# Counting out background matmuls per round: a constant count against an estimate of the round's other matmul work

## The chip, the cores and the metric

The kernel runs on one core of a Trainium2 chip. The metric is the device time of one execution in microseconds (us). Engines: PE is TensorE, which multiplies matrices (its weight loads are listed as PEld), DVE is VectorE, ACT is ScalarE, POOL is GpSimd, SP issues DMAs.

## What is computed

One layer of a hybrid encoder over 1040 tokens (16 meta tokens and 1024 others) of width 1024. A root-mean-square norm is followed by one input projection to 5920 columns, whose columns feed three branches: neighbourhood attention (8 heads), a chunked gated linear attention (GLA, 4 heads, both directions) and RWKV-7 time mixing (8 heads, both directions). The branches are concatenated, go through one output projection and are added to the input; a last norm follows.

```python
hn = rms_norm(h, norm_g[l])
z_na  = hn @ w[:, :NA_COLS]
z_gla = hn @ w[:, NA_COLS:NA_COLS + GLA_COLS]
z_rw  = hn @ w[:, NA_COLS + GLA_COLS:]
...
h = h + jnp.concatenate([o_na, o_gla, o_rw], axis=-1) @ w_out[l]
```

The RWKV-7 recurrence, per head and direction, is `S = S * w + (S a) b + v k` and `y = S r`, over all tokens in order. The kernel computes it in chunks of 64 tokens.

## The kernel before

**Projection.** The input projection is cut into jobs of 128 columns. A job multiplies in three parts (high and low halves of weights and activations), so that a chunk of some 346 tokens takes 24 matmuls of 128x128 by 128x346 into one PSUM tile named `pj`, and a job with three chunks 72 (one narrow job has 48). `proj_steps` (L209) is a generator that yields after each matmul; after a chunk's last one the evacuation (`evac`) is emitted: one ACT step and, for the RWKV columns, two DVE steps into a tile `zt`, which a DMA then writes to memory. There are 34 jobs before the attention's: first the 14 of the RWKV branch with two of its gates among them, then other gates and the GLA columns. `Feed.pull(n)` (L364) advances the current job by n matmuls; when a job starts, the weights of the job after it are loaded (`weights`, L154). Every seventh matmul it also advances a small normalization (`norm`, tiles `rb` and `nps`).

**Recurrent stage.** `run` (L912) holds seven generators: chain (C), late (L), two inversions (I for full units, J for units of one chunk), rest (R), early (E) and drain. They work on 20 units: 4 pairs of heads times one unit of one chunk and four units of four chunks for each direction. Each pass of the `while` loop is called a round here. In a round every generator advances to its next yield, which emits a few matmuls and the DVE, ACT and POOL work that belongs to them; after it, a number of projection matmuls is pulled. A chain step takes three rounds (tile `c`, with `y` beside it), and one step waits for the one before; an inversion takes 13 rounds of 16 to 36 small matmuls in 16-bit (tiles `fps`, `ta`, `tb`, `eps`, `cps`), each followed by a DVE or ACT step; `late` makes, in two rounds of each unit, the products `g`, which DVE masks into `NT`, `XR` and `GR`.

Before, each of the first 12 rounds pulls 16 matmuls, each later one 8 (`QUOTA`). When the last unit is in `rest`, `swap` (L948) pulls all jobs that are left, closes the pools of the early part and replaces the jobs by three of the attention's.

**Order.** The program's scheduler orders each engine's instructions by the order of emission and by readiness. `place` (L84) adds ordering edges: a projection matmul pulled after round r stands behind the main matmuls of round r - 2 (`LA = 2`), so that it can move forward by no more than two rounds.

Of the kernel before, what the change touches and what calls it, by code (L numbers as in the profile page):

```python
# [7 lines left out]
F32 = mybir.dt.float32  # L8
# [5 lines left out]
PM = 1  # L14
YM = 2
LA, LA2, LA3 = 2, 2, 3
QUOTA, NQ, GI, OQ, GP = 8, 5, 0, 6, 1.5
F32R = mybir.dt.float32r
F16 = mybir.dt.float16
BF16 = mybir.dt.bfloat16  # L20
# [10 lines left out]
C = 64  # L31
# [44 lines left out]
def emit(ctx, tc, a, out):  # L76
# [2 lines left out]
    PS = bass.MemoryType.PSUM  # L79
    half = (slice(0, 64), slice(64, 128))  # L80

    lane = {"cur": None, "anchors": (), "seen": None}

    def place(r):  # L84
        if lane["cur"] == "pj":
            for n in lane["anchors"]:
                tc.add_manual_dep(r.ins, n, NOSYNC, reason="issue order")
        lane["seen"] = r.ins.name
        return r

    class Tensor:
        def matmul(self, *args, **kw):
            return place(nc.tensor.matmul(*args, **kw))  # L93

        def transpose(self, *args, **kw):
            return place(nc.tensor.transpose(*args, **kw))  # L96

    def hop(g, name):
        prev, lane["cur"], lane["seen"] = lane["cur"], name, None
        done = next(g, 0) == 0  # L100
        seen, lane["cur"] = lane["seen"], prev
        return done, seen
# [69 lines left out]
    with tc.tile_pool(name="xp", bufs=1) as xp, tc.tile_pool(name="px", bufs=2, space=PS) as px:  # L172
        warm = xp.tile([128, 1], F32, name="warm")
        S.activation(warm, small[:, 0:1], AF.Sqrt)
        rows = [(16, a["meta"])] + [(128, a["x"][t * 128:(t + 1) * 128, :]) for t in range(8)]
# [208 lines left out]
    src = [Feed(jobs)]  # L384
# [17 lines left out]
    nst = {}  # L402
# [337 lines left out]
    seen = {}  # L740
# [168 lines left out]
    past = []  # L909

    HPO = {}
    def run(gens, quota):  # L912
        kinds = {id(g): k for k, g in zip('CLIJRED', gens)}
        while gens:
            alive, marks = [], []
            for g in gens:
                off = HPO.get(kinds[id(g)], 0)
                if off:
                    with tc.high_priority(off):
                        done, seen = hop(g, "main")  # L920
                else:
                    done, seen = hop(g, "main")
                if not done:
                    alive.append(g)
                if seen:
                    marks.append(seen)
            gens = alive
            past.append(marks)
            lane["anchors"] = past[-1 - LA] if len(past) > LA else ()
            if len(past) % PM == 0:  # L930
                src[0].pull(quota * PM if len(past) > 12 else 16, 3 if "pool" in nst else 10 ** 6)

    def seq(*gs):
        for g in gs:
# [27 lines left out]
    ready = {k: -1 for k in "ELRIJC"}  # L962
# [64 lines left out]
    if 1:  # L1027
        lora_weights(0)
    src[0].pull(10 ** 6, FIRST)
    run([stream("C", chains, lambda u: past_("I", u) and past_("R", u)),  # L1030
         stream("L", late, gate_l),
         stream("I", invert, lambda u: past_("L", u)),
# [505 lines left out]
def build(arr):  # L1538
    import concourse.bacc as bacc
    import concourse.tile as tile  # L1540

    nc = bacc.Bacc("TRN2", target_bir_lowering=False, num_devices=1)
    aps = {k: nc.dram_tensor(f"in_{k}_dram", v.shape, mybir.dt.from_np(v.dtype), kind="ExternalInput").ap() for k, v in arr.items()}
    out = nc.dram_tensor("out_0_dram", (T, D), F32, kind="ExternalOutput").ap()
    with tile.TileContext(nc, schedule_with_timeline_sim=True) as tc, ExitStack() as ctx:
        emit(ctx, tc, aps, out)
    return nc
# [9 lines left out]
```

## Time and profile before

| | |
|---|---|
| median of 3 runs | 1490.52 us (1487.98 to 1501.66) |
| the profiled execution's own time | 1485.04 us |
| its span, first to last instruction | 1482.8 us |
| mean granted PE clock | 0.959 of full |
| PE busy | 1375.4 us, 93% of the span |
| DVE, ACT, POOL busy | 886.2, 611.5, 665.7 us |

The recurrent stage begins at about 75 us with its first rounds and its last chain step starts at 974.7 us; attention, GLA and the output projection follow. A busy share is a mean over a stretch. The granted clock is 1.00 where PE ran at full clock all the time and 0.50 where it ran at half.

### The profile page before, as it was taken

What the parts mean: (1) busy time and instruction counts of PE and PEld (TensorE: products, weight loads), DVE (VectorE), ACT (ScalarE), POOL (GpSimd) and SP (SyncE); (2) the same over time, 40 slices, a digit from 0 to 9 for tenths busy, and PEclk for the clock granted to TensorE, in tenths of its full rate; (3) what the DMA queues carried; (4) which work ended last, traced back from release to release, by engine and by line L of the source; (5) the groups of instructions that cost most, each with busy time, mean ns of one, the idle gap of its engine ahead of it and who ended that gap; (6) DMA issues with size and microseconds to landing.
All of it is one profiled execution on the core that took longest, in us unless ns stands there. A gap on an engine that the chain in (4) does not pass through costs nothing. (4 is left out here: it accounts for less than half of the span.)

```text
span 1482.8 us, 36124 instructions
## 1 busy us (share of the span) xinstructions
PE 1375.4 (93%) x14656; PEld 1132.4 (76%) x14656; DVE 886.2 (60%) x1936; ACT 611.5 (41%) x1368; POOL 665.7 (45%) x775
## 2 busy tenths in 40 slices
PE   5888988999899999999999999998999989899997
PEld 4877777877788788788888888776677767667786
DVE  7425465676856565746656564546757577775554
ACT  5324243334443443434334332435465554644333
POOL 6435364464646664657656563223323132321223
PEclk9999898999989999999999999999999999899999
DMA  7655533433433444334333433155353423731432
GB/s 205 162 134 134 133 95 86 123 91 71 117 95 88 113 89 121 86 91 113 87 106 80 100 99 78 44 115 134 84 120 87 112 73 96 240 111 55 132 93 93
DMA packets 184806, 158.88 MB, mean 107 GB/s; under 512 B 19152, under 2 KB 168048, under 8 KB 184640
## 3 DMA queue, kind: packets, MB, share of 16 engines
q1 hardware_dynamic: 119616, 117.12, 26.6%
q0 software_dynamic: 63264, 35.20, 13.2%
q10 hardware_dynamic: 1760, 4.26, 0.8%
q8 instruction: 115, 1.88, 0.5%
q14 instruction: 51, 0.42, 0.1%
HBM read 123.81 MB, written 32.72 MB: 106 GB/s over the span
## 5 line engine op out<-in xcount | busy, mean ns | idle before, releaser
L93 PE MATMUL pj<-hhi,whi 128*128 128x348 f32 (+10 forms) x1088 | 378.9, 349 | 12.4 <-DVE zt L263 8.7
L93 PE MATMUL pj<-hlo,whi 128*128 128x348 f32 (+10 forms) x1088 | 377.0, 347 | 0.0
L93 PE MATMUL pj<-hhi,wlo 128*128 128x348 f32 (+8 forms) x1064 | 368.6, 347 | 1.7 <-POOL wlo L166 1.7
L93 PEld LDWEIGHTS pj<-hhi,whi 128*128 128x128 f32 (+1 forms) x1088 | 212.1, 195 | 28.2 <-issue 11.9
L93 PEld LDWEIGHTS pj<-hlo,whi 128*128 128x128 f32 (+1 forms) x1088 | 212.0, 195 | 12.9 <-issue 2.6
L93 PEld LDWEIGHTS pj<-hhi,wlo 128*128 128x128 f32 x1064 | 208.9, 196 | 14.4 <-issue 2.6
L166 POOL TENSOR_TENSOR wlo<-wraw,whi 128x512 fp32r<-128x512 f32 x94 | 125.6, 1337 | 144.6 <-DMA whi<-in_w_in_dram 53.6
L162 POOL DMA_DIRECT2D whi<-in_w_in_dram x94 | 74.7, 795 | 114.7 <-PE pj L93 101.3
L1219 POOL TENSOR_SCALAR sc<-sc,rc 128x288 f32<-128x288 f32 (+3 forms) x64 | 45.4, 710 | 163.9 <-DVE rc L1218 136.8
L845 POOL TENSOR_TENSOR dS<-SV,dec 64x128 f32<-64x128 f32 x128 | 59.1, 462 | 73.7 <-DVE SV L861 68.3
L699 POOL TENSOR_TENSOR BK<-BK,dec 64x1024 f32<-64x1024 f32 (+1 forms) x40 | 68.4, 1710 | 49.1 <-PE g L93 45.6
L791 ACT CAST XA<-ta 128x512 f16<-128x512 f32 (+1 forms) x92 | 49.9, 542 | 90.5 <-PE ta L93 87.3
L785 DVE TENSOR_TENSOR Fc<-fps,im 128x512 f16<-128x512 f32 (+1 forms) x92 | 58.5, 636 | 47.7 <-PE fps L93 43.6
L93 PE MATMUL ops<-hhi,oh 128*128 128x512 f32 x256 | 86.8, 403 | 0.0
L93 PE MATMUL g<-XR,BK 64*128 64x128 f32 (+1 forms) x544 | 67.6, 296 | 5.5 <-DVE GR L687 5.5
L93 PEld LDWEIGHTS g<-XR,BK 64*128 64x128 f32 x544 | 53.9, 192 | 16.5 <-issue 12.3
L1211 DVE CUSTOM_DVE_ANT_0 sc<-sps,bt 128x288 f32<-128x288 f32 (+3 forms) x64 | 33.3, 520 | 44.8 <-PE sps L93 30.4
L1328 DVE TENSOR_TENSOR yv<-ops,yv 128x512 f32<-128x512 f32 x48 | 33.0, 690 | 41.5 <-PE ops L93 41.3
L93 PEld LDWEIGHTS ops<-hhi,oh 128*128 128x128 f32 x256 | 48.6, 191 | 11.9 <-issue 1.0
L861 DVE TENSOR_TENSOR SV<-c,dS 64x128 f32<-64x128 f32 x128 | 36.7, 286 | 35.0 <-PE c L93 32.6
L257 ACT ACTIVATE zt<-pj,cols 128x347 f32<-128x347 f32 (+1 forms) x42 | 23.0, 549 | 82.5 <-PE pj L93 74.0
L93 PEld LDWEIGHTS <-Nh 64*64 64x64 f16 x1600 | 43.4, 111 | 15.0 <-issue 12.8
(302 smaller groups left out, 3048.7 us busy)
## 6 DMA issues: line engine op xcount, KB each, us to landing
whi<-in_w_in_dram POOLq DMA_DIRECT2D x94, 256.0 KB, 4.0
wraw<-in_w_in_dram SPq DMA_DIRECT2D x94, 256.0 KB
lr<-rwl POOLq DMA_DIRECT2D x32, 256.0 KB, 3.5
rwz<-zt SPq DMA_DIRECT2D x12, 544.0 KB
orr<-oscr SPq DMA_DIRECT2D x96, 64.0 KB
wr<-in_w_out_dram SPq DMA_DIRECT2D x12, 512.0 KB
glz<-zt SPq DMA_DIRECT2D x8, 544.0 KB
k<-rwz SPq DMA_DIRECT2D x32, 128.0 KB
```

What stands on the lines that cost most here:

```text
L93: return place(nc.tensor.matmul(*args, **kw))
L162: G.dma_start(out=hi, in_=w_v[:, q:q + 4, c0:c0 + 128])
L166: G.tensor_tensor(out=lo, in0=raw, in1=hi.bitcast(F32), op=ALU.subtract)
L257: S.activation(zt[:, PAD + n0:PAD + n1], ps[:, n0 - lo:n1 - lo], AF.Copy, scale=c1)
L699: G.tensor_tensor(out=bk, in0=bk, in1=dec[es, :, :, None, None].broadcast_to([64, 2, ns, 2, C]), op=ALU.mult)
L785: V.tensor_tensor(out=Fc, in0=fps, in1=mskt(l), op=ALU.mult)
L791: S.copy(A, aps)
L845: G.tensor_tensor(out=dS[es], in0=cur[es, :, e, :], in1=dcur[es, :, None].broadcast_to([64, 2, C]), op=ALU.mult)
L861: V.tensor_tensor(out=nx[es, :, e, :], in0=cps[es, 2], in1=dS[es], op=ALU.add)
L1211: V.tensor_tensor_reduce(out=sc[:, 0:m], in0=sps[:, 0:m], in1=bias[e][:, 0:m], scale=1.0, scalar=-3.0e38, op0=ALU.add, op1=ALU.max, accum_ ...
L1219: NE.tensor_scalar(out=sc[:, 0:m], in0=sc[:, 0:m], scalar1=rc, scalar2=0.5, op0=ALU.mult, op1=ALU.mult)
L1328: V.tensor_tensor(out=o, in0=ps, in1=o, op=ALU.add)
```

## The change

The pull at the end of a round gets its count from an estimate. Every matmul and transpose that goes through the wrapper class adds to `lane["work"]` its estimated time in ns: columns times passes (4 for 32-bit operands) over 2.3, halved where the array is half used, plus 3. The sum is set to zero when a round starts, so that at the pull it holds the round's other matmul work. The number of projection matmuls is what is missing to 2050 ns (2700 ns until the chain has done unit 3), at 155 ns each, and at least 4. The constant of 8, and that of 16 in the first 12 rounds, go. No instruction is added to the program or taken from it.

```diff
 LA, LA2, LA3 = 2, 2, 3
-QUOTA, NQ, GI, OQ, GP = 8, 5, 0, 6, 1.5
+FILL = 650
+QUOTA, NQ, GI, OQ, GP = 2050, 5, 0, 6, 1.5
...
-    lane = {"cur": None, "anchors": (), "seen": None}
+    lane = {"cur": None, "anchors": (), "seen": None, "work": 0.0}
...
+    def cost(st, mv, passes):
+        rows, n = mv.shape[0], int(np.prod(mv.shape[1:]))
+        shared = 2 if rows <= 64 or int(np.prod(st.shape[1:])) <= 64 else 1
+        lane["work"] += n * passes / 2.3 / shared + 3
+
     class Tensor:
         def matmul(self, *args, **kw):
+            cost(kw["lhsT"], kw["rhs"], 4 if kw["rhs"].dtype == F32 else 1)
             return place(nc.tensor.matmul(*args, **kw))
 
         def transpose(self, *args, **kw):
+            cost(kw["in_"], kw["identity"], 1)
             return place(nc.tensor.transpose(*args, **kw))
...
         while gens:
             alive, marks = [], []
+            lane["work"] = 0.0
...
-            if len(past) % PM == 0:
-                src[0].pull(quota * PM if len(past) > 12 else 16, 3 if "pool" in nst else 10 ** 6)
+            want = quota if ready["C"] >= 3 else quota + FILL
+            src[0].pull(max(round((want - lane["work"]) / 155), 4), 3 if "pool" in nst else 10 ** 6)
```

## Rows read from the trace of the kernel before

**Rows 1.** The page, part 1: busy us, share, instructions.

```profile
PE 1375.4 (93%) x14656; PEld 1132.4 (76%) x14656; DVE 886.2 (60%) x1936; ACT 611.5 (41%) x1368; POOL 665.7 (45%) x775
```

**Rows 2.** Windows: stretch, length, PE PEld DVE ACT POOL busy (count), PEclk, DMA.

```profile
75.00:129.00 54.00, 43.62 (x243) 40.74 (x240) 18.12 (x43) 12.29 (x30) 18.46 (x28) 0.91 0.62 149
129.00:185.00 56.00, 49.74 (x405) 44.58 (x406) 29.24 (x57) 18.62 (x40) 27.74 (x30) 0.88 0.47 114
185.00:241.00 56.00, 49.74 (x704) 42.09 (x702) 33.87 (x55) 23.63 (x52) 31.93 (x33) 0.91 0.36 89
241.00:354.00 113.00, 105.02 (x1589) 89.60 (x1586) 73.75 (x156) 42.69 (x101) 62.69 (x80) 0.97 0.43 105
354.00:458.00 104.00, 94.47 (x1236) 80.30 (x1232) 67.45 (x126) 44.80 (x84) 52.71 (x59) 0.89 0.36 94
458.00:890.00 432.00, 420.03 (x6242) 354.57 (x6243) 263.54 (x528) 167.25 (x364) 264.13 (x305) 0.98 0.39 98
890.00:945.00 55.00, 54.80 (x814) 47.88 (x814) 23.77 (x59) 14.91 (x35) 20.36 (x28) 1.00 0.27 64
945.00:985.00 40.00, 36.75 (x283) 28.59 (x279) 21.38 (x48) 16.16 (x31) 8.49 (x12) 1.00 0.29 67
```

**Rows 3.** Windows, PE's work on tile pj alone: stretch, length, busy (count).

```profile
75.00:129.00 54.00, 40.81 (x218) 0.91 0.62 149
...
458.00:890.00 432.00, 215.00 (x1074) 0.98 0.39 98
```

**Rows 4.** Tile c, first matmuls of a chain step: ns, first and last start.

```profile
L93 PE MATMUL c<-SV,XR x544: 222/222/367, 128.9 to 974.7; 128*64 128x64 f32 x182
```

**Rows 5.** Timeline of PE: start, us, instruction, [idle before].

```profile
507.35 0.69 PE L93 MATMUL c<-SV,KT 128*64 128x64 f32 x8 [1.22 <-DVE SV L853]
...
508.86 0.49 PE L93 MATMUL pj<-hhi,whi 128*128 128x346 f32 x1
509.15 0.49 PE L93 MATMUL pj<-hlo,whi 128*128 128x346 f32 x1
...
511.53 0.32 PE L93 MATMUL pj<-hhi,wlo 128*128 128x346 f32 x1
511.69 0.33 PE L93 MATMUL pj<-hhi,whi 128*128 128x346 f32 x1
```

**Rows 6.** Waits of PE, 75 to 130 us: total, times, longest.

```profile
PE pj L93 <- DVE zt L263: 6.5, 2, 3.5
```

**Rows 7.** Waits of PE, 129 to 354 us: total, times, longest.

```profile
PE c L93 <- DVE SV L853: 5.0, 3, 2.3
PE g L93 <- DVE GR L687: 4.8, 3, 3.5
```

**Rows 8.** Groups of DVE by line, 458 to 890 us.

```profile
L785 DVE TENSOR_TENSOR Fc<-fps,im 128x512 f16<-128x512 f32 (+1 forms) x52 | 33.3, 642 | 29.9 <-PE fps L93 26.3 <-PE xps L96 2.8 <-PE ta L93 0.2
...
L684 DVE TENSOR_TENSOR XR<-g,rmask 64x256 f32<-64x256 f32 (+1 forms) x44 | 17.0, 386 | 0.8
L682 DVE TENSOR_TENSOR NT<-g,nmask 64x256 f32<-64x256 f32 (+1 forms) x44 | 16.9, 384 | 18.1 <-PE g L93 17.7
L687 DVE TENSOR_TENSOR GR<-g,rmask 128x256 f32<-128x256 f32 x36 | 14.9, 416 | 0.3
```

**Rows 9.** Windows of two single rounds, columns as in the stage table.

```profile
675.60:677.20 1.60, 1.60 (x45) 1.40 (x43) 0.75 (x2) 0.00 (x0) 0.40 (x2) 1.00 0.65 198
830.60:831.70 1.10, 1.10 (x47) 1.03 (x48) 0.62 (x2) 0.30 (x2) 1.02 (x2) 1.00 0.06 15
```

**Rows 10.** Chain of waits at the swap: start, us, what.

```profile
914.44 3.94 PE pj L93 x24
```

**Rows 11.** Timeline of PE at the stage's end.

```profile
978.34 0.45 PE L93 MATMUL y<-GR,SV 128*64 128x64 f32 x8
...
980.90 0.30 PE L93 MATMUL pj<-hhi,wlo 128*128 128x320 f32 x1
983.48 0.50 PE L93 MATMUL vr<-fhi,hsum 128*128 128x512 f32 x1 [2.27 <-ACT fhi L538]
```

## Prediction

> **What bounds the kernel now.** I read the page first: TensorE (PE) is busy 93% of the span [rows 1]. That alone does not say where a gain can be, so next comes the table by stage [rows 2]. The changed code runs in the recurrent stage, from about 75 to 985 us. In its second half PE has hardly any idle time: 432.00 - 420.03 = 12.0 us in 458 to 890, clock 0.98. In its first half it has more: 6.3 + 6.3 + 8.0 = 20.5 us in 129 to 354, and 9.5 us in 354 to 458, with clocks of 0.88 to 0.97. The engines that feed it are far from full there (DVE 29.24 of 56 us). So the stage is bound by PE's work plus what PE loses to gaps and to the lower clock.
>
> What a projection matmul (pj) costs is read from the timeline [rows 5]: 0.16 us from start to start at full clock, 2.4 GHz (511.53 to 511.69), 0.29 us at half clock, 1.2 GHz (508.86 to 509.15); before these slow ones PE had sat idle 1.22 us for DVE. So a microsecond at half clock loses 1 - 0.16/0.29 = 0.45 us of work.
>
> **Rounds.** All counts below follow from the loops and gates of the code; the trace is only a check. The inversion of a full unit takes 13 rounds (1 + 2 x 5 + 2 yields), its chain 12, and one group of five units comes 58 rounds after the one before; the stage has 264 rounds, in both kernels, because no gate waits for a projection job in either. The check: 68 chain steps of 8 records make the 544 of [rows 4]; the first is in round 20, the last in round 258, so a round takes (974.7 - 128.9)/238 = 3.55 us.
>
> **The change part by part.**
>
> 1. *What is moved.* The new count is round((want - work)/155), at least 4; want is 2700 through round 73 (the chain of unit 3 ends there) and 2050 after. Examples: products for the inversion alone, 32 x 16.9 = 541, give (2050 - 541)/155 = 10; with a chain step's first matmuls (469) 1010, hence 7; a round with a set of "g" products, 1468, gets 4. Summed over the rounds: rounds 1 to 12 pull 201 and not 192, rounds 13 to 73 726 and not 488, rounds 74 to 235 1137 and not 1296. The jobs then run out in round 235, where before 24 were pulled in rounds 236 to 238 and the last 64 at the swap. So 247 pj matmuls (9 + 238) go from later to earlier, 247 x 0.16 = 40 us of PE time, and none is added or removed. If PE never waited, the time would not change at all. Everything hangs on idle time and clock.
>
> 2. *Estimate against real.* In 458 to 890 (rounds 100 to 235, 136 rounds with a mean estimate of 994) pj takes 215 of PE's 420.03 us [rows 2, 3]; the other 205 us stand against 136 x 0.994 = 135 estimated. The estimate is too low by a factor of 1.5, so the formula evens the rounds out only in part. An estimated 1468 is some 2.2 us.
>
> 3. *Gaps in rounds 20 to 73 (129 to 354 us), 20.5 us.* They are waits of main matmuls for DVE [rows 7], and a round has now 11 to 17 pj to lay before such a matmul instead of 8, 0.5 to 1.4 us more. Round by round, a gap can shrink by no more than the pj added in its own round: done over the chain's rounds, this covers 5 us. A pj may also move up to two rounds; the most is all 20.5. I take half, **-10** (bounds 0 and -20.5).
>
> 4. *Clock in the same stretch.* Half clock for 2 x (0.12 x 56 + 0.09 x 56 + 0.03 x 113) = 30 us [rows 2], 0.45 of it lost: 13.6 us. If half of the gaps go, half of this goes: **-6.5** (bounds 0 and -13.6).
>
> 5. *Rounds 74 to 99 (354 to 458).* 8 pj become 7 on average, light rounds get up to 13, heavy ones 4. **0** (bounds -5, half the idle time there; +6, if the thinned rounds wait as below).
>
> 6. *Rounds 100 to 235.* In rounds 74 to 235, 92 rounds lose 213 pj (34 us) and 24 gain 54. A thinned round gets shorter as long as nothing else sets its length. Single rounds of 1.1 and 1.6 us with PE wholly busy exist [rows 9], while every new round holds 2.5 us and more, so the plain dependencies of a round fit. The exception is a "g" round: DVE makes 2 x (0.384 + 0.386 + 0.416) = 2.4 us of masks from it, and 0.64 for the inversion [rows 8], and 0.3 to 0.6 for the chain, 3.3 to 3.6 us; PE has 2.2 + 4 x 0.16 = 2.85 us. At up to 0.6 us each, 22 such rounds (two for each of 11 full units) are 13 us. DVE can catch up in the rounds between, so I take **+5** (bounds -5, which is less than half of the 12 us idle there now; +34, all that is removed).
>
> 7. *The swap.* Before, 64 pj stand here in long runs, 24 of them in 3.94 us [rows 10], and with the 24 of the rounds ahead they cover the closing of the stage. Now rounds 236 to 239 have none. Their main work, estimated 740 to 1227, is some 1.1 to 1.8 us each, so about 1 us a round may be bare: **+3** (bounds 0 and +8, two rounds' worth).
>
> 8. *The tail.* The projection of the next stage's first keys lasts before until 980.9 us: 8 pj behind the last chain matmul fill the wait for the last head sums, and still 2.27 us are idle [rows 11]. Now these jobs end in round 260, so 8 x 0.16 = **+1.3** (bounds 0 and +3).
>
> The counting is host code and issues nothing. No DMA is added; weight loads of the early jobs come sooner, in the same order on their queues, and the load share falls from 0.62 in 75 to 129 us to 0.36 in 185 to 241 [rows 2], which leaves room for jobs that come half as fast again.
>
> Sum: -10 - 6.5 + 0 + 5 + 3 + 1.3 = -7.2 us. On the profiled execution's 1485.04 us this is 1478. That execution lies 5.5 us under the median of the runs, 1490.52, so for a median I predict 1490.5 - 7.2 = **1483 us**.
>
> **The rivals.**
>
> *Faster by over 1%: the early gaps close almost wholly.* For it: the added 238 pj are 38 us of cover against 20.5 us of gaps, and each closed gap can save its slow stretch too. Against it: a gap of 3.5 us [rows 7] is longer than what one round adds. With -16, -11, -5, +2, +1, +1 the sum is -28: 1462.
>
> *Slower: thinned rounds wait for DVE.* One mechanism, in rounds 74 to 235: what PE no longer does there it spends waiting. At its full price, +34 in place of +5, the sum is +22: 1512. It makes the change a loss from +12 on, and a loss of over 1% from +27, 80% of the pj removed. For it: DVE's 3.3 to 3.6 us of a "g" round. Against it: only 22 of the 92 rounds are "g" rounds, and the one-round rows of [rows 9]. The Trainium skill (Perfetto Trace Analysis, "Identifying the Most-Contended Engine") says that matmul busy time is a bad measure of how near PE is to its limit, and that weight-load busy time should be taken. By that measure PE is 354.57/432 = 82% full where its matmul row says 97% [rows 2], and a fifth of these rounds would be latency that stays when pj leave; that speaks for this rival.
>
> *No gain from the early rounds: evacuation binds.* The extra pj wait for their own PSUM buffers, as in 75 to 129 us, where PE idles 10.4 us over 218 pj [rows 2, 3], 6.5 of them for the last step of an evacuation [rows 6]. At that rate 238 pj cost 11 us, and item 3 becomes about +1: the sum is +4, 1494. Against it: there 16 pj a round came with hardly any other matmul between; now there is some 1.2 us of other work in each round.
>
> *The change does not do what it says.* The program's scheduler may place pj by readiness, whatever a round's count. Against it: the pj of the timeline stand in blocks of 8. It would give about 1488.
>
> **How the numbers follow.** I give 0.30 to the gaps closing (1462), 0.19 to thinned rounds waiting (1512 at most, a loss of over 1% only at its upper end and with the swap), and 0.51 to my sum with the two cases near it (1483, 1488, 1494). The likeliest case has 1483, and a range of its own of 1473 to 1498. About 1% is what a measurement of this kernel can tell from no change: under 1475.6 is faster, over 1505.4 slower. Faster is the first rival, 0.30. Of the slower rival 0.17 lies beyond 1505.4. The rest, 0.53, is no change. For 8 in 10 the range goes from 1462 to 1508; some 0.08 lie under it and 0.10 above.
>
> **What would show it.** Items 3 and 4 are right if idle time in the rounds up to the fourth chain's end falls to about 10 us and the clock there rises to 0.94 or more, while the stretch itself gets longer by some 20 us (38 added, 16 saved). Item 6 is right if the stretch of rounds 100 to 235 gets shorter by some 15 to 20 us at no more than 17 us of idle time; it is wrong, and the slower rival right, if PE's waits for the masks (GR, NT) and the chain's copies grow by tens of us there. The swap shows as PE idle between the last job's matmuls and the first of the next stage; the evacuation rival as waits of pj for zt. What would upset all: a scheduler that orders later stages another way.

## The result, and the profile after

The changed kernel has a median of 1506.62 us against 1490.52 us, a ratio of 1.011 [1.0082, 1.0139]: slower by 1.1%, where 1483 us and no measurable change had been forecast; the time lies just under the upper end of the range, 1508, which it owes to the width of that range: the forecast had the other sign. One of its 13 executions took 1996.55 us at a mean granted clock of 0.555; this slow one is left out of the ratio. The profiled execution of the changed kernel took 1505.52 us (before 1485.04), its span is 1503.7 us (1482.8). So the two traces differ by 20.9 us, 4.8 more than the medians do.

The amount of work is the same. Part 1 of the page of the kernel after answers to [rows 1]: PE is busy 1379.5 us, 4.1 more than before, in a span that is 20.9 longer.

```profile
PE 1379.5 (92%) x14656; PEld 1137.1 (76%) x14656; DVE 899.2 (60%) x1936; ACT 610.9 (41%) x1368; POOL 666.1 (44%) x775
```

To find the place, both traces are cut at the same rounds. Windows of the kernel after: rounds up to 20 (first chain step), 20 to 75, 75 to 100, 100 to 236, 236 to 249, 249 to 258. The columns are those of [rows 2].

```profile
75.00:126.00 51.00, 41.70 (x238) 39.02 (x238) 18.45 (x41) 12.03 (x28) 18.44 (x28) 0.93 0.65 157
126.00:396.30 270.30, 248.32 (x3025) 217.79 (x3024) 157.52 (x301) 98.71 (x217) 140.43 (x163) 0.96 0.45 111
396.30:480.70 84.40, 79.31 (x1153) 65.70 (x1152) 53.23 (x96) 36.28 (x71) 51.18 (x58) 0.94 0.36 93
480.70:907.30 426.60, 401.89 (x6078) 340.61 (x6072) 267.19 (x529) 163.12 (x357) 251.09 (x291) 0.96 0.36 91
907.30:948.00 40.70, 39.33 (x656) 33.85 (x655) 21.92 (x53) 12.64 (x29) 15.22 (x23) 0.92 0.20 47
948.00:987.80 39.80, 37.37 (x313) 29.75 (x312) 18.45 (x43) 12.00 (x25) 9.18 (x11) 0.96 0.25 59
```

The same, PE's work on tile pj alone, answering to [rows 3] (rounds 20 to 75, 75 to 100, 100 to 236, 236 to 258):

```profile
126.00:396.30 270.30, 160.47 (x841) 138.91 (x841) 32.50 (x58) 17.57 (x35) 0.96 0.45 111
396.30:480.70 84.40, 36.14 (x175) 27.66 (x174) 0.50 (x1) 3.94 (x9) 0.94 0.36 93
480.70:907.30 426.60, 190.25 (x938) 151.53 (x938) 10.10 (x20) 17.57 (x39) 0.96 0.36 91
907.30:987.80 80.50, 42.94 (x208) 34.75 (x207) 7.63 (x17) 6.84 (x18) 0.94 0.23 53
```

And the kernel before, cut at the same rounds (20 to 75, 100 to 236, 236 to 249):

```profile
128.90:361.80 232.90, 210.76 (x2770) 181.62 (x2769) 140.58 (x277) 87.75 (x197) 124.53 (x146) 0.93 0.42 102
...
458.50:889.90 431.40, 419.43 (x6238) 354.25 (x6238) 263.54 (x528) 167.08 (x364) 263.99 (x305) 0.98 0.39 98
889.90:944.60 54.70, 54.50 (x807) 47.66 (x806) 23.37 (x57) 14.52 (x34) 20.07 (x27) 1.00 0.28 65
```

In these windows the projection matmuls (pj) moved as counted. What each stretch gained or lost is its change in length less 0.16 us for each pj that came or went (pj, idle time and half clock here and below are worked out from all of PE's records and from the granted clock in a stretch):

| rounds | length before, after | pj before, after | net | PE idle | half clock |
|---|---|---|---|---|---|
| up to 20 | 53.9, 51.0 | 216, 216 | -2.9 | 10.4 to 9.3 | 10.2 to 6.8 |
| 20 to 75 | 232.9, 270.3 | 592, 841 | -2.4 | 22.1 to 22.0 | 34.1 to 20.5 |
| 75 to 100 | 96.7, 84.4 | 200, 174 | -8.1 | 7.9 to 5.1 | 20.5 to 10.2 |
| 100 to 236 | 431.4, 426.6 | 1072, 938 | **+16.6** | 12.0 to 24.7 | 17.1 to 34.1 |
| 236 to 258 | 84.6, 80.5 | 271, 207 | +6.1 | 0.8 to 3.8 | 0 to 10.2 |
| 258 to the first attention scores | 22.8, 21.1 | 73, 48 | +2.3 | 2.7 to 4.2 | 3.4 to 6.8 |
| attention to the end | 485.6, 494.8 | 576, 576 | +9.2 | 29.5 to 33.6 | 30.0 to 47.2 |

Rounds 100 to 236 lost 134 pj, 21.4 us of work, and became 4.8 us shorter. PE's idle time doubled: 426.60 - 401.89 = 24.7 us against 431.40 - 419.43 = 12.0. The time at half clock doubled too; at 0.45 of it lost, idle time and clock together account for 12.7 + 7.7 = 20 us, a little more than the 16.6. That stretch is most of the loss. A second trace of each kernel, below, gives +14.7 there; up to round 100 the traces of one kernel differ more, by up to 10 us at half clock.

What PE waits for there, in the waits of the kernel after, rounds 100 to 236 (total, times, longest):

```profile
PE ta L100 <- DVE Fc L793: 8.9, 7, 4.1
PE lo L100 <- DMA lr<-rwl: 2.7, 2, 1.4
PE xps L104 <- DVE XU L779: 2.6, 4, 1.8
PE v L104 <- DVE GR L695: 2.1, 1, 2.1
...
PE g L100 <- DVE GR L695: 1.2, 1, 1.2
PE t L104 <- DVE GR L695: 1.1, 1, 1.1
```

And the first of them in the kernel before, same rounds:

```profile
PE ta L93 <- DVE Fc L785: 1.3, 3, 0.5
```

The greatest is an inversion's mask `Fc`, made by DVE from `fps`. The waits for the masks of `g` (`GR`), which I had feared, are 4.4 us together against 2.3 before. The longest wait is seen in two timelines. PE:

```profile
530.83 0.34 PE L100 MATMUL y<-XR,SV 64*64 64x64 f32 x6
535.28 0.63 PE L100 MATMUL ta<-Fc,XU 64*64 64x64 f16 x16 [4.11 <-DVE Fc L793]
...
537.01 0.49 PE L100 MATMUL pj<-hlo,whi 128*128 128x346 f32 x1
537.29 0.49 PE L100 MATMUL pj<-hhi,wlo 128*128 128x346 f32 x1
```

And DVE in the same microseconds:

```profile
529.97 1.31 DVE L657 SCALAR_TENSOR_TENSOR al<-al,kn 128x128 f32<-128x128 f32 x1 [0.99 <-ACT BK L655]
531.21 1.81 DVE L730 SCALAR_TENSOR_TENSOR r<-r,hc,k 128x512 f32<-128x512 f32 x1
533.05 0.29 DVE L855 TENSOR_SCALAR U<-c 128x128 f32<-128x128 f32 x1
533.26 1.39 DVE L641 TENSOR_TENSOR_SCAN Sd<-smask,Sd 128x64 f32<-128x64 bf16 x2
534.57 0.66 DVE L793 TENSOR_TENSOR Fc<-fps,im 128x512 f16<-128x512 f32 x1
```

`Fc` itself takes 0.66 us, but it stands behind 4.6 us of other DVE work: 0.3 us are the chain's `U`, the rest is element-wise preparation (`al`, `r`, the scan `Sd`) that PE doesn't wait for here. DVE is busy only 267.19 of 426.60 us in this stretch, 63%: it isn't full, its queue is in the wrong order for this moment. And the pj that follow run 0.28 us apart, at half clock.

### The profile page after: what moved, and what is told of

The parts are those of the page before. It is cut to its first block, busy times and chain, and to the rows that moved or that the text cites. A ratio compares the mean times of both kernels' runs of the same rounds, so it can differ in the third digit from the quotient of the medians.

```text
span 1503.7 us, 36113 instructions
## 1 busy us (share of the span) xinstructions
PE 1379.5 (92%) x14656; PEld 1137.1 (76%) x14656; DVE 899.2 (60%) x1936; ACT 610.9 (41%) x1368; POOL 666.1 (44%) x775
## 4 chain that ended last, share of the span: by engine, by line
PE 52%; DVE 9%; POOL 3%; ACT 3%; issue 3%; DMA 3%; SPq 0%; DVEq 0%; POOLq 0%; ACTq 0%
PE pj L100 17%; PE ops L100 10%; PE c L100 3%; PE o_ps L100 3%; PE sps L100 2%; PE y L100 2%; PE g L100 2%; PE tps L104 2%; PE dps L100 1%; DVE Sd L641 1%; PE ta L100 1%; PE lo L100 1%; PE fps L100 1%; PE t L104 1%; PE tb L100 1%
## 5 line engine op out<-in xcount | busy, mean ns | idle before, releaser
L690 DVE TENSOR_TENSOR NT<-g,nmask 64x256 f32<-64x256 f32 (+1 forms) x80 | 30.4, 380 | 46.4 <-PE g L100 45.4
L1225 ACT ACTIVATE sc<-sc,nm 128x288 f32<-128x288 f32 (+3 forms) x64 | 37.6, 587 | 50.3 <-DVE nm L1223 50.1
```

The lines of the kernel that those rows point to most:

```text
L1225: S.activation(sc[:, 0:m], sc[:, 0:m], AF.Exp, bias=nm, accum_out=sm)
```

## The experiments

**The theories**, with the letters that the expectations use. V, thin rounds: by the evening-out, rounds with much other work lose the pj that covered their waits for DVE. F, early move: the pj moved forward close no gap, and the later rounds, 7 on average, wait. S: the rounds around the swap, now empty, do the harm. D: DVE's queue ahead of the inversion is the cause. And one formed after the first four experiments, P, place: it isn't the amount in a round that counts but in which rounds the chunks (24 pj, then an evacuation) end. With 8 per round a chunk takes exactly three rounds, so that its ends come every third round and there are three places for them; with the estimate the ends wander.

A chain step takes three rounds too, and the expectations speak of the place against these. That part does not hold: the chain stands still between units, and a group of 58 rounds is no multiple of three. In the trace of the kernel before, of the 45 evacuations in rounds 100 to 236, 15 begin behind the first matmuls of a chain step, 21 behind the second and 9 behind the third. A place is a set of rounds of the program, not a phase of the chain step.

A table of all profiles, rounds 100 to 236, comes after them. A ratio compares with executions of the kernel before made beside that run (their medians are 1489 to 1491 us); its 95% interval stands in brackets. A stretch comes from one trace each. First the kernel before and the one after were run again:

> The kernel before once more, for a second profile. If the 11.9 us of PE idle time in rounds 100 to 235 belong to its order of instructions, they come again within 2 us, and the attention stage (first sps matmul to the end, 485.6 us) shows how much it scatters.

It took 1487.07 us. In rounds 100 to 236: 431.9 us, 12.1 idle, against 431.4 and 12.0.

> The changed kernel once more, for a second profile. All theories: about 1506 us. If the 9 us that the attention stage took longer in the first profile belong to the change, they come again (from the first sps matmul to the end 494 us or more, against 485.6 before); if they are scatter of the clock, this part takes another time.

1510.27 us, 1.0117 [1.0078, 1.0156]; 425.2 us, 23.9 idle. So the idle time there belongs to the program's order of instructions; it isn't scatter, and nor is the half clock, 17.1 and 34.1 us as in the first pair. The attention stage took 489.1 and 494.8 us in these two.

**Constants that do the same move, without the estimate.**

```diff
-            if len(past) % PM == 0:
-                src[0].pull(quota * PM if len(past) > 12 else 16, 3 if "pool" in nst else 10 ** 6)
+            n = 16 if len(past) <= 12 else quota if "pool" in nst else 12 if ready["C"] < 3 else 7
+            src[0].pull(n, 3 if "pool" in nst else 10 ** 6)
```

> Front-loading alone, by constants: 16 in the first 12 rounds as before, then 12 a round until the chain has done unit 3, then 7, and 8 after the swap. The estimate is not used. The jobs run out at the swap as in the changed kernel. Theory F (front-loading does the harm: the extra matmuls of the early rounds close no gap, and rounds with a mean of 7 wait for DVE): about 1505 us, with PE idle time in rounds 100 to 235 of 20 us or more. Theory V (the evening-out does it: rounds with much other work, in which DVE has most to do, lose their cover): about 1490 us, idle time there as before, 12 us. Theory S (the empty rounds around the swap do it): about 1496.

1505.09 us, 1.0116 [1.0078, 1.0154], as much as the change itself, with 29.3 us idle in rounds 100 to 236, as theory F had it. So the loss comes without the estimate too.

**The estimate alone, with nothing moved early** (`FILL` out, 16 in the first 12 rounds, 2175 ns so that the sum of the counts stays):

```diff
+            n = max(round((2175 - lane["work"]) / 155), 4) if len(past) > 12 else 16
+            src[0].pull(n, 3 if "pool" in nst else 10 ** 6)
```

> Evening-out alone: the count by the estimate, with 2175 ns in every round from the 13th on and 16 matmuls in the first 12, so that the mean stays near 8 and 59 matmuls are left at the swap (64 before). Theory F: as before, about 1490 us. Theory V: about 1503 us, with PE idle time of 20 us or more in rounds 100 to 235 against 12. Theory S: as before, 1490.

1509.51 us, 1.0148 [1.0115, 1.0181]. Rounds 100 to 236 hold 1049 pj, only 23 fewer than before, and take 20.3 us longer, with 28.1 us idle, as theory V had it. So such a loss needs neither the early move nor a lack of pj in sum. Each half of the change alone costs as much as both together.

**An early move of 64 pj, so that nothing is left for the swap:**

```diff
+            n = 16 if len(past) <= 12 else 9 if len(past) <= 76 else quota
```

> The empty swap alone: 9 instead of 8 in rounds 13 to 76, so that no matmul is left at the swap; else the constants of before. Theory S: 1496 us or more, the loss lying between round 236 and the end of the stage. Theories F and V: within 3 us of before (64 matmuls, 10 us, move from the swap to the early rounds).

1496.28 us, 1.0053 [1.002, 1.0086]. The time is the one of theory S, but the loss lies elsewhere. The swap loses nothing: rounds 236 to 258 take 71.9 us with about 72 fewer pj than before's 84.6, net -1. Rounds 20 to 100 even gain 12 us net. But rounds 100 to 236, with 8 per round and the 1072 pj of before, take 454.5 us instead of 431.4. This led to the theory of the place: 64 is not a multiple of 24, so the chunks now end in other rounds.

**The place alone.** One round of 16 fewer, or one more, shifts the chunk ends by a round and moves 8 pj:

```diff
-                src[0].pull(quota * PM if len(past) > 12 else 16, 3 if "pool" in nst else 10 ** 6)
+                src[0].pull(quota * PM if len(past) > 11 else 16, 3 if "pool" in nst else 10 ** 6)
```

> The constants of before, but 16 matmuls in the first 11 rounds and not 12: every later projection chunk ends one round later against the recurrent work; 72 matmuls are left at the swap (64 before). Theory P (the loss comes from where the projection's chunks and evacuations fall against the rounds, and before has a lucky place): PE idle time in rounds 100 to 235 rises from 12 to 20 us or more, 1496 us or more. Theories F and V (thinned rounds): idle time there 12 us, and time as before, 1490.

1491.51 us, 1.0023 [0.9998, 1.0048]; rounds 100 to 236 take 441.3 us, 19.3 of them idle. The idle time is nearly that of theory P, but the time is that of the others: no loss in the whole is shown.

With `> 13` in place of `> 11`:

> The constants of before, but 16 matmuls in the first 13 rounds: chunks end one round earlier than before, the third of the three places (before and the job-ahead run have the first: 11.9 and 17.1 us of idle time in rounds 100 to 235; minus 8 and the empty swap have the second: 19.3 and 22.8). Theory P: another idle time there, most likely 18 us or more, and 1492 us or more. If places don't matter: 12 us and 1490.

1500.68 us, 1.0071 [1.0047, 1.0095]; 444.3 us, 18.1 idle, as theory P had it. Both shifts cost 10 to 13 us in that stretch; only the second shows in the whole time.

**One job ahead at the old place.** Eight pj more than in the 64-pj move make 72, three chunks, so that the ends stay:

```diff
+            n = 16 if len(past) <= 12 else 9 if len(past) <= 84 else quota
```

> The constants of before, but 9 in rounds 13 to 84: from round 85 on the projection is ahead by exactly 72 matmuls, one job, so that chunk ends fall on the same rounds as before, with another job's work behind them; nothing is left at the swap. Theory P: idle time in rounds 100 to 235 is near 12 us again, and the time 1485 to 1490 us. If it stays at 20 us or more, as in the run with 9 in rounds 13 to 76 (22.8), the place of the chunks is not the cause.

1480.78 us, 0.9933 [0.9908, 0.9959], against 1.0053 for the run with 64. Eight matmuls more moved, of 3240 pj in the kernel, make 1.2% of the time. Rounds 100 to 236 take 434.2 us, with 17.1 us idle, between the 12 of theory P and the 20 that would have spoken against it. Rounds 20 to 100 take 326.2 us with 72 pj more than before's 329.6: -14.9 net.

**The change's evening-out with the chunk ends held.** The estimate again, but every third round pulls what is missing to 24:

```diff
+            n = min(max(round((2175 - lane["work"]) / 155), 4), 20 - lane["block"])
+            if len(past) <= 12:
+                n = 16
+            elif "pool" in nst:
+                n = 8
+            elif len(past) % 3 == 0:
+                n, lane["block"] = 24 - lane["block"], 0
+            else:
+                n = min(n, 16) if len(past) % 3 == 1 else n
+                lane["block"] += n
```

> Evening-out with the chunks kept in place: the count follows the estimate (2175 ns), but every three rounds together pull exactly 24, so that each projection chunk ends in the same round as before. The run with the free estimate took 1509.5 us with 28 us of PE idle time in rounds 100 to 235. Theory P (the place of the chunk ends against the three rounds of a chain step makes the loss): idle time there back to 12 to 18 us and 1485 to 1495 us. Theory V (rounds with much other work lose their cover): idle time stays above 22 us and the time above 1500.

1493.68 us, 1.0013 [0.999, 1.0036], where the free estimate of the same target had 1.0148. Idle time in rounds 100 to 236 falls from 28.1 to 19.7 us, a little above what theory P had; the time is as it had it. So most of the estimate's loss goes when the chunk ends are held, although single rounds still pull 4 to 14. But this edit also levels the sum: three rounds together pull 24 always, with the free estimate 15 to 31. That thinness over several rounds does the harm, and not the ends, is a rival that no run here separates. The change itself lets the ends loose in the same way, with 134 pj fewer in the stretch; it was not run with its early move and the ends held together. And evening the rounds out gains nothing even when they are held.

**DVE's queue.** The changed kernel with one product of the preparation on POOL instead of DVE:

```diff
-            (G if 0 else V).tensor_tensor(out=XR[es, :, :, 2 * e, :], in0=exc[es], in1=kn[es], op=ALU.mult)
+            (G if 1 else V).tensor_tensor(out=XR[es, :, :, 2 * e, :], in0=exc[es], in1=kn[es], op=ALU.mult)
```

> The changed kernel with the two products exc x kn of each unit (the first step of late) on POOL and not on DVE. Theory D (PE waits in the thinner rounds because DVE has long element-wise steps queued ahead of the inversion's masks): PE idle time in rounds 100 to 235 falls from 24 to 16 us or less, and the time to about 1498 us. Otherwise idle time stays at 24 or the waits move to POOL, and the time is 1506 or more.

1494.21 us, 1.0021 [0.9998, 1.0043]: 12 us better than the change without it. In rounds 100 to 236 the wait for `Fc` falls from 8.9 to 1.3 us, as theory D had it:

```profile
PE v L104 <- DVE GR L695: 6.3, 3, 2.2
...
PE ta L100 <- DVE Fc L793: 1.3, 2, 0.8
```

But other waits grow, idle time falls only from 24.7 to 20.4 us (theory D: 16 or less), half clock rises from 34.1 to 61.4 us, and the stretch takes 429.0 us instead of 426.6. The gain of this trace lies in rounds 20 to 100 (354.7 to 346.4 us) and in the attention stage (494.8 to 485.0), which the edit doesn't touch. So the queue makes that wait, but relieving it did not shorten the stretch where most of the loss lies. The same edit on the run that is one job ahead:

> The job-ahead run (9 in rounds 13 to 84) with the products exc x kn on POOL instead of DVE. Theory D (DVE's queue is what the chain waits for): faster than the job-ahead run's 1481, about 1473. If DVE matters only where chunks fall badly: 1481 again.

1497.19 us, 1.0039 [1.0011, 1.0066], 16 us worse than without it and outside both expectations, at 16.0 us idle but 68.3 us at half clock. So relieving DVE is not a cure in general; it gives another order, which may be better or worse.

**Other ways to be one job ahead.** 12 in rounds 13 to 30:

```diff
+            n = 16 if len(past) <= 12 else 12 if len(past) <= 30 else quota
```

> One job ahead, but earlier: 12 in rounds 13 to 30 (two rounds a chunk), then 8, so that from round 31 on the chunks end in the same rounds as before. Theory P: as the run with 9 in rounds 13 to 84, about 1481 us. Theory F (front-loading itself does harm): slower than before, 1495.

1476.28 us, 0.9891 [0.9858, 0.9923]. And 16 in the first 21 rounds, one constant of the kernel before changed from 12 to 21:

> One constant changed: 16 matmuls in the first 21 rounds and not 12, then 8. One job ahead from round 22 on, chunks at the first place. If the place decides: 1476 to 1481 us, as the two other runs that are one job ahead. If the early rounds cannot take 16 a round for so long (waits for the evacuation, as in 75 to 129 us): 1485 or more.

1472.99 us, 0.9889 [0.9852, 0.9926], the lowest median of the study; its ratio can't be told from the run before it. All three kernels that move 72 pj keep rounds 100 to 236 at 433 to 436 us. In rounds 20 to 100 they and the 64-pj run gain 12 to 18 us net, where the kernel after, with 223 pj more there, gained 8 to 11 and the constants 3: in these traces a small early move gains more there than a large one.

**Are the evacuations what makes the place?** The 64-pj and the 72-pj run, both with the evacuations of gate and GLA columns cut to 8 columns (a part of the activations is written to memory in their place):

```diff
-            o = zt[:, n0 - 16:n1 - 16]
+            o, ps = zt[:, n0 - 16:n0 - 8], ps[:, 0:8]
...
-        nc.sync.dma_start(out=dst, in_=zt[:, 0:T])
+        nc.sync.dma_start(out=dst, in_=flat_h[:, 0:T])
```

> The run with the empty swap (9 in rounds 13 to 76, chunks at the second place, 454.5 us in rounds 100 to 235) with the evacuation of gates and GLA jobs cut to 8 columns of each chunk; what they write is then not the projection but a part of the normalized input. If the evacuations' work on ACT and DVE is what costs at this place: about 432 us there. If it is not: 450 us or more.

> The job-ahead run (9 in rounds 13 to 84, chunks at the first place, 434.2 us in rounds 100 to 235) with the same evacuations cut to 8 columns and the same part of the input written in place of the projection. If the evacuations are what costs: as the run at the second place, about 430 us; otherwise some 20 us less than that run.

1504.96 us, 1.012 [1.0076, 1.0165], and 1514.47 us, 1.0185 [1.014, 1.0229]. Rounds 100 to 236 now take 445.9 and 445.0 us, so neither expectation came. The difference between the two places (454.5 and 434.2) is gone, but halfway: the better place is worse by 11 us, with less work to do. Both also took 20 to 25 us longer up to round 20 than the runs without the edit, with 284 pj there in place of 242 and 223. Less evacuation work gave another order everywhere. That the difference hangs on the evacuations is therefore not shown; it stays a possibility.

The windows of rounds 100 to 236 of the experiments, in the order before again, after again, the constants, the estimate alone, 64 moved, 8 fewer, 8 more, one job ahead, chunk ends held, POOL on after, POOL on one job ahead, 12 early, 21 rounds, and the two with short evacuations:

```profile
457.00:888.90 431.90, 419.81 (x6240) 354.36 (x6238) 265.07 (x528) 166.91 (x364) 263.15 (x305) 0.98 0.39 98
486.50:911.70 425.20, 401.27 (x6082) 340.38 (x6074) 266.93 (x529) 163.25 (x357) 251.23 (x291) 0.96 0.36 92
488.80:921.70 432.90, 403.61 (x6093) 341.39 (x6090) 275.66 (x532) 164.26 (x358) 252.91 (x292) 0.96 0.35 90
462.10:913.80 451.70, 423.62 (x6193) 360.54 (x6186) 274.08 (x526) 166.43 (x362) 260.05 (x301) 0.94 0.37 93
460.20:914.70 454.50, 431.67 (x6242) 368.75 (x6238) 264.07 (x529) 167.09 (x363) 261.75 (x303) 0.94 0.37 93
454.00:895.30 441.30, 422.01 (x6270) 359.00 (x6264) 261.59 (x529) 168.34 (x367) 263.72 (x309) 0.97 0.39 97
456.30:900.60 444.30, 426.17 (x6214) 360.40 (x6207) 267.92 (x527) 167.88 (x363) 258.08 (x302) 0.96 0.38 95
452.90:887.10 434.20, 417.11 (x6212) 354.49 (x6208) 268.43 (x528) 166.31 (x363) 262.69 (x302) 0.98 0.39 97
453.90:891.90 438.00, 418.32 (x6208) 356.95 (x6205) 266.19 (x528) 166.89 (x363) 261.14 (x305) 0.97 0.39 97
476.30:905.30 429.00, 408.62 (x6080) 349.57 (x6074) 244.97 (x504) 165.27 (x357) 270.75 (x314) 0.93 0.36 91
452.90:906.90 454.00, 438.03 (x6214) 372.34 (x6212) 247.51 (x502) 168.84 (x363) 281.30 (x324) 0.92 0.37 92
453.20:886.60 433.40, 416.98 (x6209) 354.62 (x6206) 268.52 (x528) 166.12 (x363) 261.49 (x299) 0.98 0.40 98
450.30:885.80 435.50, 419.32 (x6212) 356.83 (x6206) 264.30 (x528) 166.30 (x363) 261.09 (x299) 0.97 0.39 97
475.70:921.60 445.90, 427.29 (x6266) 364.08 (x6262) 260.11 (x529) 156.03 (x365) 261.23 (x303) 0.96 0.33 78
477.20:922.20 445.00, 425.46 (x6216) 361.39 (x6208) 265.59 (x528) 155.46 (x363) 260.43 (x299) 0.95 0.33 77
```

The reader takes the first two figures of a line (length less PE busy is idle time) and the clock near its end. Worked out from the same traces, with the first place for the one of before, second and third for 8 fewer and 8 more:

| kernel | ratio | chunk ends | pj | length | idle | gaps of 1 us or more | half clock |
|---|---|---|---|---|---|---|---|
| before | 1 | first | 1072 | 431.4 | 12.0 | 5 | 17.1 |
| after | 1.011 | wander | 938 | 426.6 | 24.7 | 10 | 34.1 |
| constants 12, 7 | 1.0116 | wander | 938 | 432.9 | 29.3 | 12 | 30.7 |
| estimate alone | 1.0148 | wander | 1049 | 451.7 | 28.1 | 11 | 54.6 |
| estimate, ends held | 1.0013 | first | 1071 | 438.0 | 19.7 | 7 | 23.9 |
| 72 moved: 9s, 12s, 21 rounds | 0.9933, 0.9891, 0.9889 | first | 1072 | 434.2, 433.4, 435.5 | 17.1, 16.4, 16.2 | 6, 6, 8 | 17.1, 17.1, 23.9 |
| 8 fewer | 1.0023 | second | 1080 | 441.3 | 19.3 | 7 | 27.3 |
| 64 moved | 1.0053 | second | 1072 | 454.5 | 22.8 | 10 | 54.6 |
| 8 more | 1.0071 | third | 1072 | 444.3 | 18.1 | 7 | 37.5 |

At 8 per round the first place takes 431 to 436 us in four kernels, the others 441 to 455 in three, with hardly a pj between them. That two kernels at the second place lie 13 us apart shows that the place is not the whole of it. Nor does it account for all of the loss: ends that wander should meet the three places about equally, and the mean of the three is some 442 us (an estimate from these rows), while the three kernels with wandering ends, brought to 1072 pj at 0.16 us each, take 448 to 455.

## Why the prediction was wrong

**What bounds it, and the counts (items 1 and 2): right.** The 249 pj more in rounds 20 to 75, the 160 fewer in 75 to 236 and the 89 fewer after them are the 238, 159 and 88 counted. PE's work stayed what it was, and all was decided by idle time and clock, as said there. Some readings are off, though little hangs on them: the loop makes 263 passes, not 264; rounds 20 to 73 pull 7 to 17 pj by the formula, not 11 to 17; rounds 74 to 99 at most 10, not 13; and of the 20 "g" rounds of full units in rounds 100 to 235 eight pull 6, not 4.

**The rival that the change has no effect** falls with this: the scheduler moved them as counted.

**Item 3 (early gaps, -10): wrong.** The idle time of rounds 20 to 75 did not fall (22.1 and 22.0 us). The step that failed is the half between 5 and 20.5: the gaps changed their place, and did not fill. The stretch grew by 37.4 us, not by some 20. The waits of PE of the kernel after in these rounds show them:

```profile
PE ta L100 <- DVE Fc L793: 6.7, 4, 3.6
PE pj L100 <- DVE zt L342: 3.8, 1, 3.8
PE fps L100 <- DVE XA L785: 3.4, 2, 2.4
```

Of [rows 7] the wait for `GR` has gone and that for `SV` nearly; `Fc` has grown from 2.9 us, and one wait of 3.8 us for pj's own buffer has come. The rival of the evacuation was seen in that one wait, not as 11 us.

**Item 4 (clock, -6.5): right in one pair of traces, not in the other.** Half clock in rounds 20 to 75 fell from 34.1 to 20.5 us, and 0.45 of 13.6 is 6.1 us; but in the second pair from 27.3 to 23.9, 1.5 us. So half clock in this stretch differs between executions of one kernel by 3 to 7 us. The mean clock rose from 0.93 to 0.96, the sign that was named, although the idle time stayed, which I had tied together.

**Item 5 (rounds 74 to 99, 0): outside its bounds.** Rounds 75 to 100 gave -8.1 us (second pair -7.1), with 5.1 us idle instead of 7.9 and less half clock. Items 3 to 5 together gave -10.6 (second pair -7.9) where -16.5 was forecast.

**Item 6 (rounds 100 to 235, +5): the step that failed and decided.** It measured +16.6 (second pair +14.7). The bound of +34 held, but my reason for a value near the lower end was wrong: I reckoned how much DVE work a thinned "g" round holds against PE's in that round, as if only the amounts in a round mattered. The waits that grew are for the inversion's `Fc`, 0.64 us of DVE work that I had counted; the 4.6 us in front of it in DVE's queue were in no round's sum. That the chunk ends decide how such work falls is argued from the runs with shifted ends, not seen in a trace; and in the run with the constants and the one with the estimate alone `Fc` takes only 4 us of the 28 to 29 idle, the rest lies in many other waits. The test named in the prediction, no more than 17 us idle, was missed with 24.7.

**The slower rival: right in stretch and engine, wrong in mechanism.** PE waits for DVE there, but the sign that the prediction gave for it did not come: waits for `GR` grew by 2 us, those for the chain's copies fell, and nothing grew by tens of us. Single thin rounds are not enough for the loss: with the ends held, the estimate alone loses nothing that can be measured. Thinness over several rounds is not ruled out. The weight-load measure of the Trainium skill (Perfetto Trace Analysis, "Identifying the Most-Contended Engine"), which spoke for it, agrees with the trace as far as it goes: 340.61/426.60 = 80% after, 82% before, and removing work did not shorten the stretch by that work. It doesn't tell the places apart: 81% in the 64-pj run (454.5 us), 82% in the 72-pj one (434.2).

**Items 7 and 8 (+3 and +1.3): signs right, sizes low.** +6.1 for rounds 236 to 258 and +2.3 behind them. Rounds 236 to 258 are mostly clock: 10.2 us at half clock, none before. Yet the swap needs no cover: the 64-pj run and the first of the 72-pj runs left nothing for it, and net of the pj gained and lost 1 us there.

**Not in the sum.** The stretch up to round 20 gained 2.9. The attention stage, which the change doesn't touch, took 494.8 us in both traces of the kernel after, against 485.6 and 489.1. In five traces PE's instructions stand in the same order from there on (before twice, 8 more, one job ahead, POOL on one job ahead), and they took 485.6 to 493.2 us: so 7.6 us of difference come without any change in that order. In the kernel after the order is another one; what it adds to this scatter stays open.

The sum by what was measured: -2.9 - 10.6 + 16.6 + 6.1 + 2.3 = +11.5 us in the stage, and 9.2 behind it.

**What stays open:** why one set of rounds for the chunk ends is better than another, how much of the change's own loss is the place and how much is thinness, and why the shortened evacuations cost time. The kernel before may simply have a lucky place.

## What to carry to other kernels

When filler work on a saturated engine runs beside a chain of dependent steps, its count also sets the rounds in which its own side work, here the evacuations, comes up. A constant that divides a chunk evenly keeps these rounds fixed; an adaptive count lets them wander. Before making the count adaptive, shift it by one round and by a whole number of chunks: here one constant, 13 or 21 in place of 12, gave 1.007 and 0.989 of the time. And a bound by amounts per round misses a queue: look at what stands in front of the instruction that the engine waits for. Then look whether relieving that wait shortens the stretch; here it did not.

## What the hardware did that was not expected

**Short gaps and the clock.** In rounds 100 to 236 of the kernel before PE had 5 gaps of 1 us or more, and all four of its stretches at half clock began in such a gap or shortly behind it; of the changed kernel's 10 gaps six were followed so, and all six of its stretches came that way. It isn't always so: in the second trace of the changed kernel one of seven began 15 us behind a gap, and in the run one job ahead with a product on POOL the longest of all, 17.1 us from 719.0, began with no such gap in the 137 us before it. In these traces the others lasted from 3 to 14 us. Idle time alone doesn't tell how much: the run one job ahead had 17.1 us idle and 17.1 us at half clock, the same with a product on POOL 16.0 and 68.3, and took 20 us longer for it.

**The same DVE product at two speeds.** The product that the POOL runs moved, two 64-partition operands of 512 columns, took 0.67 to 1.73 us in one kernel. From the line's record of the kernel after, rounds 100 to 236 (ns, least, median, most):

```profile
L672 DVE TENSOR_TENSOR XR<-E1f,kn x20: 672/799/1732, 481.6 to 901.7; 64x512 f32<-64x512 f32 x20
L672 DVE TENSOR_TENSOR XR<-E1m,kn x4: 401/881/1674, 535.1 to 726.3; 64x128 f32<-64x128 f32 x4
```

Of the 64 in the kernels before and after only three had POOL idle beside them, and these took 0.67 to 0.69 us (at 251.8 and 252.5 us of the kernel before, 269.4 of the one after). Every one over 1 us had POOL busy for at least 0.65 of it, but many fast ones had POOL busy too. The Trainium skill (GPSIMD Engine Reference, "Specifications") says that POOL shares its SBUF interfaces with DVE, with contention when a DVE instruction has two SBUF inputs, as this product has. The trace fits that as a condition, though three are few; which POOL instruction does it, no run here separates.
